# A two-layer DiT block on one core: layer 0's expert rows written to two tables instead of added up in DRAM, with the order of pools and of some small steps changed

## The chip, the cores and the metric

One core of one Trainium2 chip runs the whole program in a single launch. The metric is the device time of that launch in microseconds (us). Before the change three runs took 2960.69, 2967.70 and 2971.63 us; the median is 2967.70 us.

## What is computed

The reference is a diffusion transformer of two layers over 512 image tokens and 256 context tokens of 1024 elements. Each layer is a mixer (retention, window attention and global attention on one wide input product, merged by a gated product) and a mixture of 16 experts of which each token takes two. Six vectors made from the conditioning by a product (shift, scale and gate, twice) modulate both halves. The part that the change is about, shortened:

```
def reference(...):
    for l in range(2):
        mod = silu(c) @ w_mod[l] + b_mod[l]          # image tokens
        mod_c = silu(c_ctx) @ w_mod[l] + b_mod[l]    # context tokens
        sh1, sc1, gt1, sh2, sc2, gt2 = split(mod, 6)
        h = rms_norm(x, g_norm1[l]) * (1 + sc1) + sh1
        hc = rms_norm(ctx, g_norm1[l]) * (1 + csc1) + csh1
        y, yc = mixer_sublayer(h, hc, ...)
        x = x + gt1 * y                              # and ctx in layer 0
        h = rms_norm(x, g_norm2[l]) * (1 + sc2) + sh2
        x = x + gt2 * moe_ffn(h, ...)                # and ctx in layer 0
    return rms_norm(x, g_final)

def moe_ffn(tokens, ...):                            # two experts of one group for each token
    contrib = expert(tokens[t]) * weight             # 2 rows for each token
    return zeros_like(tokens).at[t].add(contrib)
```

## The kernel before

All work is on one core, and each engine works through its instructions in the order in which the program emits them: TensorE (PE) the products, ScalarE (ACT) and VectorE (DVE) the elementwise work, GpSimd (POOL) small statistics, some adds and the indirect DMAs, SyncE (SP) nearly all other DMAs. A wait of one instruction therefore holds up everything behind it on its engine or queue. The 768 tokens are six tiles of 128 (0 to 3 image, 4 and 5 context). A full-precision product is three reduced ones: a weight chunk `raw` (128 x 1024, 512 KB) is cast to `wh` by ACT (L102), DVE makes the rest `wl` (L114), and both `raw` and `xH`/`xL` parts are multiplied (`mm3`). `ws.pump(n)` starts the next n chunks of a fixed list of weights: the load (L83), the cast and the subtraction are emitted where it is called.

Layer 0 ends with its experts. An expert's rows of one block, scaled, are in a tile `yo`; `add_up` (L1667) sends them by an indirect DMA from POOL that adds each row to the token's row of `yd` in DRAM. `yd` has been filled with zeros in layer 0's mixer (six memsets on POOL, six stores on SP, L1134). After the experts comes a loop with a number of turns that is only known on the chip (`For_i`, L1950); no instruction is moved across it. The statement ahead of the loop pumps the 4 x 3 pages of three modulation blocks and two chunks of layer 1's first weights, and then finishes the last expert (`b.finish()`: scale, scatter).

After the loop stands the part that the rows below are about, in this order:

- `fillers(TURN)`: three blocks (1,4), (1,5), (1,6) of layer 1's modulation: products `modps` into four groups of 32 PSUM partitions each (24 matmuls), whose parts (two rows each) DVE adds, four 2 x 512 adds a block (L439). These adds wait in a list `conts` and are emitted by layer 1's mixer. Their results go to DRAM later (`held`).
- `mixer(1)` begins. `n1_load(m)` loads token tile m: `x` (page of pool `kv`, from `xa`) and `y` (page of pool `ot`, from `yd`). `n1_sum(m)` makes x + gt2 * y on DVE (L630, L631) and stores x to `xb` for image tiles (L633, SP). `n1_stat(m)`: sum of squares on ACT (L492), root on POOL (L486, L487). `n1_scale(m)`: ACT (L642). `n1_put(m)`: PE turns the tile (`h1t`, L648), ACT (L665) and DVE (L667) scale and shift it, writing back into the pages of `x` and `y`, and L670/L672 split it into `hH`, `hL`.
- The first product, block AK, goes over the six token tiles (`psAK`); ahead of tile i its step `n1_before` puts tile i+1, loads tile i+5, scales i+2, and takes the statistics of i+3; the sum of tile i+4 is behind it.

Pools of a mixer are opened in the order kv, pp, ot, hp and lie on one another's addresses of the stage before in that order. At the end of layer 1 `last(m)` scales the output tiles: one DVE operation a tile (L1976) with `gf`, the final gain, loaded just ahead of them. A half-width expert block of layer 1 scales its result in two operations of 64 partitions (L1793), since its two halves belong to different columns of the gate row.

Of the kernel before, what the change touches and what calls it, by code (L numbers as in the profile page):

```python
# [16 lines left out]
D = 1024  # L17
# [135 lines left out]
def tile_dit(ctx, tc, a, out):  # L153
# [49 lines left out]
    yd = dram.tile([6 * 128, D], F32, name="yd")  # L203
# [150 lines left out]
    sc0 = small([128, 8, 32], F32, "sc0")  # L354
    jp = pool0.tile([128, 128], I32, tag="pg", name="jp")
# [9 lines left out]
    nc.vector.memset(ones, 1.0)  # L365

# [40 lines left out]
    def mod_gen(l, n, pool, tag, hold=None):  # L407
# [5 lines left out]
        def two():  # L413
            t = pool.tile([2, 1024], F32, tag=tag, name=f"mb{l}_{n}")
            return t[:, 0:512], t[:, 512:1024]

        r, gt = two()
# [8 lines left out]
        ps = acc_tile("modps") if (l, n) in TURN[2:] else oac_tile("modps")  # L426
# [35 lines left out]

        conts.append(fin)
# [12 lines left out]
    held, gt2 = [], []  # L476
# [119 lines left out]
    def mixer(l):  # L596
        att = ExitStack()
        kv = att.enter_context(tc.tile_pool(name=f"kv{l}", bufs=5))
        pp = att.enter_context(tc.tile_pool(name=f"pp{l}", bufs=6))
        ot = att.enter_context(tc.tile_pool(name=f"ot{l}", bufs=4))  # L600
        hp = att.enter_context(tc.tile_pool(name=f"hp{l}", bufs=HP))
# [8 lines left out]
        pages, rs = {}, {}  # L610

        def n1_load(m, first=False):
# [72 lines left out]
        if l:  # L685
# [6 lines left out]
            conts.pop(0)()  # L692
            conts.pop(0)()
# [3 lines left out]
            conts.pop(0)()  # L697
            assert not conts
            n1_sum(1)
            n1_put(0)  # L700
# [3 lines left out]
            n1_stat(1)  # L704
            n1_scale(1)
            n1_sum(2)
# [408 lines left out]
        def soft_gen():  # L1115
# [11 lines left out]
            for i in range(len(steps) + 1):  # L1127
# [509 lines left out]
    def moe(l, R, late, ex, x0):  # L1637
# [284 lines left out]
        for s in range(NE):  # L1922
# [494 lines left out]
```

## Time and profile before

| | |
|---|---|
| median of three runs | 2967.70 us |
| the profiled execution's own time | 2957.83 us |
| its span in the profile | 2956.0 us |
| mean granted TensorE clock | 0.975 of full speed |
| PE busy | 2770.4 us (94%) |
| DVE busy | 1820.3 us (62%) |
| ACT busy | 1279.6 us (43%) |
| POOL busy | 366.2 us (12%) |

PE is busy nearly all the time, so what matters are the few stretches in which it is not. Times in the trace count from the span's start. A timeline row gives the start, the length, engine, line, operation, output and input names, shapes, how many instructions the row joins, and in brackets the idle time of the engine ahead of it with what ended it.

### The profile page before, as it was taken

How to read it: one execution, taken by the hardware profiler on the slowest of the kernel's cores; microseconds unless marked ns; L12 is line 12 of the kernel's file. 1: busy time of each engine (PE TensorE's matmuls, PEld its weight loads, DVE VectorE, ACT ScalarE, POOL GpSimd, SP SyncE). 2: the span in 40 equal slices, each digit the busy share in tenths (PEclk: the TensorE clock that was granted, in tenths of full speed). 3: DMA queues.
4: the chain of work that ended last, by engine and by line, in shares of the span. 5: the costliest groups of instructions: out<-in, count | busy, mean ns of one | idle time of the engine just before them, and what ended most of it. 6: DMA issues, size and time to landing. Idle time of an engine off the chain costs nothing. (4 is left out here: it accounts for less than half of the span.)

```text
span 2956.0 us, 42080 instructions
## 1 busy us (share of the span) xinstructions
PE 2770.4 (94%) x15253; PEld 2221.1 (75%) x15253; DVE 1820.3 (62%) x3235; ACT 1279.6 (43%) x2376; POOL 366.2 (12%) x427
## 2 busy tenths in 40 slices
PE   7999999999999999979999599999999999989985
PEld 3788888888887767767777378888988887767652
DVE  4675567666554455668676576667676655668443
ACT  4444445445443211218566354444455442226332
POOL 1220000000011000023222131100000100012211
PEclk9999999999999999989999799999999999989998
DMA  6433222213243566769999732222223447689997
GB/s 242 132 109 105 90 76 87 95 65 105 99 155 122 194 242 254 263 239 323 340 356 361 254 119 90 83 87 92 72 97 127 143 151 289 214 315 335 372 368 287
DMA packets 203765, 557.63 MB, mean 189 GB/s; under 512 B 27014, under 2 KB 51718, under 8 KB 203552
## 3 DMA queue, kind: packets, MB, share of 16 engines
q1 hardware_dynamic: 175680, 502.59, 47.5%
q0 software_dynamic: 10752, 25.03, 3.4%
q10 hardware_dynamic: 17120, 27.27, 2.5%
q8 instruction: 121, 1.98, 0.3%
q14 instruction: 92, 0.75, 0.1%
HBM read 461.95 MB, written 96.77 MB: 189 GB/s over the span
## 5 line engine op out<-in xcount | busy, mean ns | idle before, releaser
L114 DVE TENSOR_TENSOR wl<-raw,wh 128x1024 fp32r<-128x1024 f32 x474 | 565.3, 1221 | 139.4 <-ACT wh L102 136.2
L102 ACT CAST wh<-raw 128x1024 fp32r<-128x1024 f32 x474 | 484.4, 1050 | 353.7 <-DMA raw<-oT 106.3
L892 ACT ACTIVATE P<-sc,st 128x768 f32<-128x768 f32 (+4 forms) x240 | 176.5, 735 | 339.8 <-DVE st L890 213.3
L890 DVE TENSOR_REDUCE st<-sc 128x1 f32<-128x768 f32 (+4 forms) x240 | 178.6, 744 | 118.9 <-PE sc L179 113.2
L926 ACT CAST ptH<-pt 128x512 fp32r<-128x512 f32 x264 | 143.0, 592 | 124.0 <-PE pt L911 103.3
L179 PE MATMUL psb<-wl,wh 128*128 128x512 f32 x480 | 189.1, 394 | 6.5 <-DVE wl L114 6.5
L179 PE MATMUL psb<-wh,wh 128*128 128x512 f32 x480 | 192.6, 401 | 0.3 <-ACT wh L102 0.3
L179 PE MATMUL psb<-wh,wl 128*128 128x512 f32 x480 | 188.7, 393 | 2.1 <-DVE wl L114 2.0
L936 DVE TENSOR_TENSOR ptL<-pt,ptH 128x512 fp32r<-128x512 f32 x264 | 169.6, 681 | 9.3 <-ACT ptH L926 7.3
L911 PE MATMUL pt<-ident,P 128*128 128x128 f32 x1056 | 141.4, 275 | 14.7 <-ACT P L892 11.8
L911 PEld LDWEIGHTS pt<-ident,P 128*128 128x128 f32 x1056 | 119.7, 140 | 45.4 <-ACT P L892 31.8
L179 PE MATMUL psR<-wh,hH 128*128 128x512 f32 (+1 forms) x384 | 150.7, 392 | 0.0
L179 PE MATMUL psR<-wl,hH 128*128 128x512 f32 (+1 forms) x384 | 147.4, 384 | 3.0 <-DVE wl L114 3.0
L179 PE MATMUL psR<-wh,hL 128*128 128x512 f32 (+1 forms) x384 | 147.8, 385 | 0.0
L898 DVE TENSOR_SCALAR P<-P,st 128x768 f32<-128x768 f32 (+3 forms) x240 | 130.1, 542 | 8.5
L486 POOL TENSOR_SCALAR rstd<-ss 128x4 f32<-128x4 f32 (+2 forms) x70 | 22.6, 323 | 833.9 <-ACT h L492 354.2
L179 PEld LDWEIGHTS psb<-wh,wh 128*128 128x128 f32 x480 | 90.8, 189 | 46.0 <-issue 15.9
L179 PEld LDWEIGHTS psb<-wl,wh 128*128 128x128 f32 x480 | 91.1, 190 | 27.3 <-DVE wl L114 9.8
L179 PE MATMUL sc<-swkT,swqs 128*128 128x256 f32 x704 | 109.1, 281 | 2.2 <-ACT P L892 2.2
L179 PEld LDWEIGHTS psb<-wh,wl 128*128 128x128 f32 x480 | 90.8, 189 | 22.8 <-DVE wl L114 3.7
L1099 DVE COPY sc<-sink 128x1 f32<-128x1 f32 x160 | 25.8, 161 | 128.7 <-PE sc L179 122.5
L179 PE MATMUL yps<-wh,hidT 128*128 128x512 f32 x320 | 105.0, 399 | 0.0
(528 smaller groups left out, 6903.8 us busy)
## 6 DMA issues: line engine op xcount, KB each, us to landing
raw<-in_w_in_dram SPq DMA_DIRECT2D x136, 512.0 KB
raw<-in_w_gate_dram SPq DMA_DIRECT2D x128, 512.0 KB
raw<-in_w_up_dram SPq DMA_DIRECT2D x128, 512.0 KB
raw<-in_w_down_dram SPq DMA_DIRECT2D x128, 512.0 KB
raw<-in_w_mod_dram SPq DMA_DIRECT2D x96, 512.0 KB
raw<-in_w_br_dram SPq DMA_DIRECT2D x48, 512.0 KB
raw<-oT SPq DMA_DIRECT2D x30, 512.0 KB
raw<-in_w_out_dram SPq DMA_DIRECT2D x16, 512.0 KB
```

Of the source, the lines that this page charges most:

```text
L102: self.nc.scalar.copy(c.h, c.raw)
L114: self.nc.vector.tensor_tensor(c.l, c.raw, c.h.bitcast(F32), op=OP.subtract)
L179: nc.tensor.matmul(ps, lhs, rhs, start=start, stop=stop, skip_group_check=share)
L486: nc.gpsimd.tensor_scalar(r[:, 0:cnt], ss, four / n, four * EPS, op0=OP.mult, op1=OP.add)
L890: nc.vector.reduce_max(st[:, 1, h:h + 1], s[:, 0:self.ns], axis=AX.X, negate=True)
L892: nc.scalar.activation(self.P[h][:, 0:self.ns], s[:, 0:self.ns], AF.Exp, bias=st[:, 1, h:h + 1], accum_out=st[:, 2, h:h + 1])
L898: nc.vector.tensor_scalar(self.P[h][:, 0:self.nk], self.P[h][:, 0:self.nk], st[:, 3, h:h + 1], None, op0=OP.mult)
L911: nc.tensor.transpose(pt[:, c * 256 + h * 128:c * 256 + (h + 1) * 128], self.P[2 * x + h][:, i * 128:(i + 1) * 128], ident)
L926: nc.scalar.copy(ph, src)
L936: nc.vector.tensor_tensor(pl, src, ph.bitcast(F32), op=OP.subtract)
L1099: nc.vector.tensor_copy(s[:, nk:nk + 1], sink[:, hd:hd + 1])
```

## The change

1. `yd` has two tables of 768 rows. In layer 0 the scatter only writes: a token's first choice goes to row t of the first table, its second choice to row t of the second. The zero-fill is gone. Layer 1 is as it was.
2. Layer 1's `n1_load` also loads the tile's rows of the second table, as two 128 x 512 halves `y2`, and `n1_sum` adds them to `y`: on DVE for tile 0, on POOL for tiles 1 to 5.
3. The mixer's pools are opened in the order hp, kv, ot, pp.
4. The parts of the three late modulation blocks are copied to SBUF by ACT (128 x 512, L471) and added by one PE product with a 0/1 matrix `four` (`modsum`), so DVE has one add a block. These adds now stand after `n1_scale(1)`, not around `n1_sum(0)`. `n1_stat(1)` moves ahead of `n1_put(0)`.
5. The last expert of layer 0 is finished ahead of the pump, not behind it.
6. In layer 1 the gate row is also kept in the half blocks' layout (`gt2half`), so L1793's two operations become one. `gf` is loaded two experts earlier than the end. The final tiles are multiplied by `gf` first, then scaled by ACT and DVE in turns.

```diff
-    yd = dram.tile([6 * 128, D], F32, name="yd")
+    yd = dram.tile([2 * 6 * 128, D], F32, name="yd")
...
-        ps = acc_tile("modps") if (l, n) in TURN[2:] else oac_tile("modps")
+        ps = acc_tile("modps") if late else oac_tile("modps")
...
         def fin():
-            for i in range(4):
-                nc.vector.tensor_tensor(r, ps[32 * i:32 * i + 2, :], r, op=OP.add)
+            if late:
+                ps2 = oac_tile("modsum")
+                mm(ps2[0:2, :], four, t[:, 512:1024], True, True)
+                nc.vector.tensor_tensor(r, ps2[0:2, :], r, op=OP.add)
...
+        if late:
+            assert v not in (1, 4)
+            nc.scalar.copy(t[:, 512:1024], ps)
         conts.append(fin)
...
+        hp = att.enter_context(tc.tile_pool(name=f"hp{l}", bufs=HP))
         kv = att.enter_context(tc.tile_pool(name=f"kv{l}", bufs=5))
+        ot = att.enter_context(tc.tile_pool(name=f"ot{l}", bufs=4))
         pp = att.enter_context(tc.tile_pool(name=f"pp{l}", bufs=6))
-        ot = att.enter_context(tc.tile_pool(name=f"ot{l}", bufs=4))
-        hp = att.enter_context(tc.tile_pool(name=f"hp{l}", bufs=HP))
...
                 nc.sync.dma_start(pages[m][1], yd[m * 128:(m + 1) * 128, :])
+                for i in range(2):
+                    second[m, i] = half(f"y2{m}{i}")
+                    nc.sync.dma_start(second[m, i], yd[(6 + m) * 128:(7 + m) * 128, i * 512:(i + 1) * 512])
...
                 x, y = pages[m]
+                for i in range(2):
+                    c = slice(i * 512, (i + 1) * 512)
+                    (nc.gpsimd if m else nc.vector).tensor_tensor(y[:, c], y[:, c], second.pop((m, i)), op=OP.add)
                 nc.vector.tensor_tensor(y, y, gt2[m // NIMG], op=OP.mult)
...
-            conts.pop(0)()
-            conts.pop(0)()
             n1_sum(0)
             n1_stat(0)
             n1_scale(0)
-            conts.pop(0)()
-            assert not conts
             n1_sum(1)
+            n1_stat(1)
             n1_put(0)
             for _ in range(2):
                 ws.pump(1)
                 ws.low()
-            n1_stat(1)
             n1_scale(1)
+            assert len(conts) == len(TURN)
+            while conts:
+                conts.pop(0)()
             n1_sum(2)
...
-                if l == 0 and i < 6:
-                    z = half("zeros")
-                    nc.gpsimd.memset(z, 0.0)
-                    nc.sync.dma_start(yd[i * 128:(i + 1) * 128, :].rearrange("p (r c) -> p r c", c=512),
-                                      z[:, None, :].to_broadcast([128, 2, 512]))
...
         def add_up(yo, at, view, rows):
+            how = dict(compute_op=OP.add) if l else {}
...
-                    for n in range(2):
-                        p = slice(n * 64, (n + 1) * 64)
-                        nc.vector.scalar_tensor_tensor(yo[p, 0:512], self.y[p], w[p], gt2row[p, n * 512:(n + 1) * 512],
-                                                       op0=OP.mult, op1=OP.mult)
+                    nc.vector.scalar_tensor_tensor(yo[:, 0:512], self.y, w, gt2half, op0=OP.mult, op1=OP.mult)
...
-            if l == 0 and not nx:
-                ws.pump(4 * len(TURN) + WEND)
             ws.low()
             for b in blocks[s]:
                 b.finish()
+            if l == 0 and not nx:
+                ws.pump(4 * len(TURN) + WEND)
+                ws.low()
+            if l == 1 and s == NE - 3:
+                gf.append(pool0.tile([128, D], F32, tag="pg", name="gf"))
+                nc.sync.dma_start(gf[0], bc(a["g_final"], D))
...
     def last(m):
-        nc.vector.scalar_tensor_tensor(xt[m], xt[m], rs[m][:, 0:1], gf, op0=OP.mult, op1=OP.mult)
+        r = rs[m][:, 0:1]
+        if m % 2:
+            nc.vector.tensor_scalar(xt[m], xt[m], r, None, op0=OP.mult)
+        else:
+            nc.scalar.activation(xt[m], xt[m], AF.Copy, scale=r)
         nc.sync.dma_start(out[0, m * 128:(m + 1) * 128, :], xt[m])
 
     for m in range(NIMG):
         rs[m] = row_rstd(xt[m], y0[m])
+        nc.vector.tensor_tensor(xt[m], xt[m], gf, op=OP.mult)
```

The change moves instructions on three engines after the loop. DVE before, from the third modulation block's adds on (n11m is tile m of layer 1, its `kv` and `ot` the pages of x and y, `gt` the gate row, `mb` a modulation block):

```order
L439 TENSOR_TENSOR mb_6_15628<-modps,mb_6_15628 2x512 x4
L630 TENSOR_TENSOR n111ot<-n111ot,gt_15340 128x1024
L631 TENSOR_TENSOR n111kv<-n111kv,n111ot 128x1024
L667 TENSOR_SCALAR n110ot<-h1t_01_15706,mT_146 128x128 x4
L672 TENSOR_TENSOR hL_0_15716<-n110kv,hH_0_15715 128x512
L672 TENSOR_TENSOR hL_0_15716<-n110ot,hH_0_15715 128x512
L114 TENSOR_TENSOR wl_15738<-raw_15729,wh_15737 128x1024
L630 TENSOR_TENSOR n112ot<-n112ot,gt_15340 128x1024
L631 TENSOR_TENSOR n112kv<-n112kv,n112ot 128x1024
L630 TENSOR_TENSOR n113ot<-n113ot,gt_15340 128x1024
L631 TENSOR_TENSOR n113kv<-n113kv,n113ot 128x1024
L667 TENSOR_SCALAR n111ot<-h1t_11_15772,mT_146 128x128 x4
```

The same place of DVE in the changed kernel, from the split of tile 0 to the put of tile 1 (L682 was L667):

```order
L687 TENSOR_TENSOR hL_0_15714<-n110ot,hH_0_15713 128x512
L114 TENSOR_TENSOR wl_15736<-raw_15727,wh_15735 128x1024
L442 TENSOR_TENSOR mb_4_15599<-modsum,mb_4_15599 2x512
L449 TENSOR_SCALAR mb_4_15599<-mb_4_15599 2x512
L442 TENSOR_TENSOR mb_5_15601<-modsum,mb_5_15601 2x512
L449 TENSOR_SCALAR mb_5_15601<-mb_5_15601 2x512
L442 TENSOR_TENSOR mb_6_15613<-modsum,mb_6_15613 2x512
L645 TENSOR_TENSOR n112ot<-n112ot,gt_15324 128x1024
L646 TENSOR_TENSOR n112kv<-n112kv,n112ot 128x1024
L645 TENSOR_TENSOR n113ot<-n113ot,gt_15324 128x1024
L646 TENSOR_TENSOR n113kv<-n113kv,n113ot 128x1024
L682 TENSOR_SCALAR n111ot<-h1t_11_15784,mT_146 128x128 x4
```

The modulation adds went from ahead of the sums of tiles 0 and 1 to between the chunk's `wl` and the sum of tile 2; the sums of tiles 2 and 3 stand ahead of the put of tile 1 in both.

SP's queue before, from the loads of tile 2 to the first weight:

```order
L623 DMA n112kv<-xa_115 128x1024
L625 DMA n112ot<-yd 128x1024
L623 DMA n113kv<-xa_115 128x1024
L625 DMA n113ot<-yd 128x1024
L633 DMA xb_117<-n110kv 128x1024
L633 DMA xb_117<-n111kv 128x1024
L83 DMA raw_15729<-in_w_in_dram 128x1024
```

The same place in the changed kernel:

```order
L632 DMA n112kv<-xa_115 128x1024
L634 DMA n112ot<-yd 128x1024
L637 DMA y_15670<-yd 128x512
L637 DMA y_15672<-yd 128x512
L632 DMA n113kv<-xa_115 128x1024
L634 DMA n113ot<-yd 128x1024
L637 DMA y_15678<-yd 128x512
L637 DMA y_15680<-yd 128x512
L648 DMA xb_117<-n110kv 128x1024
L648 DMA xb_117<-n111kv 128x1024
L83 DMA raw_15727<-in_w_in_dram 128x1024
```

Sixteen loads instead of eight (tiles 0 to 3) stand ahead of the first store of x, and so ahead of the first weight.

On POOL only the pairs of the root (L486, L487) stood here before, one pair a tile. Now the second table's adds of a tile stand behind the pair of the tile before it:

```order
L496 TENSOR_TENSOR rstd<-rstd,nhalf 128x1
L644 TENSOR_TENSOR n111ot<-n111ot,y_15662 128x512
L644 TENSOR_TENSOR n111ot<-n111ot,y_15664 128x512
L495 TENSOR_SCALAR rstd<-ss 128x1
L496 TENSOR_TENSOR rstd<-rstd,nhalf 128x1
L644 TENSOR_TENSOR n112ot<-n112ot,y_15670 128x512
L644 TENSOR_TENSOR n112ot<-n112ot,y_15672 128x512
```

So POOL can begin the adds of tile m+1 only when tile m's root is done, which needs tile m's sum on DVE and its squares on ACT.

## Rows read from the trace of the kernel before

**Rows 1.** Windows: stretch, us, busy PE, PEld, DVE, ACT, POOL, clock, DMA share, GB/s.
```profile
1350.00:1650.00 300.00, 296.83 (x1566) 216.67 (x1565) 205.39 (x197) 193.89 (x220) 73.72 (x46) 1.00 0.98 350
1650.00:1700.00 50.00, 20.15 (x103) 12.43 (x104) 28.49 (x38) 18.46 (x35) 7.45 (x11) 0.66 0.65 224
...
1750.00:2450.00 700.00, 678.97 (x3994) 589.65 (x3993) 461.58 (x892) 333.17 (x694) 64.20 (x71) 1.00 0.33 110
```

**Rows 2.** Timeline of PE after the loop.
```profile
1660.44 6.72 PE L179 MATMUL modps<-raw,sc 128*32 128x512 f32 x48 [12.63 <-DMA mb<-in_b_mod_dram]
1677.20 1.97 PE L648 MATMUL h1t<-ident,n110ot 128*128 128x128 f32 x8 [10.04 <-ACT n110ot L642]
1683.24 0.79 PE L179 MATMUL psAK<-wh,hH 128*128 128x512 f32 x1 [4.07 <-ACT hH L670]
1690.18 1.97 PE L648 MATMUL h1t<-ident,n111ot 128*128 128x128 f32 x8 [5.29 <-ACT n111ot L642]
...
1704.93 0.47 PE L179 MATMUL psAK<-wh,hH 128*128 128x512 f32 x1 [0.70 <-DVE nAK L790]
```

**Rows 3.** Timeline of SP's queue after the loop.
```profile
1666.38 0.35 SPq L623 DMA_DIRECT2D n110kv<-xa  x1
...
1669.93 0.44 SPq L625 DMA_DIRECT2D n113ot<-yd  x1
1673.87 0.32 SPq L633 DMA_DIRECT2D xb<-n110kv  x1
...
1692.22 0.33 SPq L633 DMA_DIRECT2D xb<-n113kv  x1
```

**Rows 4.** Waits of SP's queue, 1640 to 1700 us: total, times, longest.
```profile
SPq L623 <- PE modps L179: 5.6, 1, 5.6
```

**Rows 5.** Timeline of DVE after the loop.
```profile
1663.81 2.84 DVE L439 TENSOR_TENSOR mb<-modps,mb 2x512 f32<-2x512 f32 x4 [9.47 <-PE modps L179]
...
1672.62 1.23 DVE L631 TENSOR_TENSOR n110kv<-n110kv,n110ot 128x1024 f32<-128x1024 f32 x1
...
1683.83 0.69 DVE L672 TENSOR_TENSOR hL<-n110ot,hH 128x512 fp32r<-128x512 f32 x1
1686.17 1.23 DVE L114 TENSOR_TENSOR wl<-raw,wh 128x1024 fp32r<-128x1024 f32 x1 [1.66 <-ACT wh L102]
...
1692.26 1.37 DVE L667 TENSOR_SCALAR n111ot<-h1t,mT 128x128 f32<-128x128 f32 x4
...
1699.12 1.23 DVE L630 TENSOR_TENSOR n114ot<-n114ot,gt 128x1024 f32<-128x1024 f32 x1 [4.11 <-DMA n114ot<-yd]
```

**Rows 6.** Timeline of ACT around and after the loop.
```profile
1652.98 0.68 ACT L1789 ACTIVATE yo<-ysm,lrec 128x512 f32<-128x512 f32 x1
...
1681.04 1.51 ACT L665 ACTIVATE n110kv<-h1t,mT 128x128 f32<-128x128 f32 x4 [3.89 <-DMA xb<-n110kv]
...
1685.10 1.04 ACT L102 CAST wh<-raw 128x1024 fp32r<-128x1024 f32 x1 [1.39 <-DMA raw<-in_w_in_dram]
```

**Rows 7.** Groups of POOL, whole span: busy us, mean ns, idle before.
```profile
L594 POOL TENSOR_TENSOR oA<-rope,rope 128x512 f32<-128x512 f32 x16 | 21.5, 1343 | 59.0 <-DVE rope L589 35.6 <-issue 12.1 <-DVE st L897 11.3
...
L487 POOL TENSOR_TENSOR rstd<-rstd,nhalf 128x1 f32<-128x1 f32 x26 | 16.2, 625 | 2.2
```

**Rows 8.** Timeline of POOL after the loop.
```profile
1699.17 1.75 POOL L487 TENSOR_TENSOR rstd<-rstd,nhalf 128x2 f32<-128x2 f32 x1
```

**Rows 9.** Timeline of the end, by DVE, SP and ACT.
```profile
2930.64 1.51 DVE L1793 SCALAR_TENSOR_TENSOR yo<-ysm,lrec,gt2row 64x512 f32<-64x512 f32 x2 [5.09 <-PE ysm L179]
...
2937.14 0.35 SPq L1969 DMA_DIRECT2D gf<-in_g_final_dram  x1
2937.54 2.46 SPq L1973 DMA_DIRECT2D cx<-xa  x4
...
2942.91 1.06 ACT L492 ACTIVATE cy<-cx 128x1024 f32<-128x1024 f32 x1 [16.39 <-DMA cx<-xa]
```

**Rows 10.** Timeline of ACT where layer 0's merge begins.
```profile
1000.86 1.05 ACT L102 CAST wh<-raw 128x1024 fp32r<-128x1024 f32 x1 [6.44 <-DMA raw<-oT]
```

More of the change, by code (lines that the diff above doesn't have):

```diff
@@ L354, in tile_dit @@
     sc0 = small([128, 8, 32], F32, "sc0")
+    four = small([128, 2], F32, "four")
     jp = pool0.tile([128, 128], I32, tag="pg", name="jp")
@@ L365, in tile_dit @@
     nc.vector.memset(ones, 1.0)
+    nc.vector.reduce_sum(four, ident.rearrange("p (i r) -> p r i", r=32)[:, 0:2, :], axis=AX.X)
     def late_consts():
@@ L411, in mod_gen @@
         v, half = divmod(n, 2)
[L413 to L417, printed above, removed]
+        late = (l, n) in TURN
+        t = pool.tile([128 if late else 2, 1024], F32, tag=tag, name=f"mb{l}_{n}")
+        r, gt = t[0:2, 0:512], t[0:2, 512:1024]
         b_ap = a["b_mod"][l, n * 512:(n + 1) * 512]
@@ L437, in fin @@
         def fin():
-            for i in range(4):
-                nc.vector.tensor_tensor(r, ps[32 * i:32 * i + 2, :], r, op=OP.add)
+            if late:
[3 more added lines that the diff above has]
+            else:
+                for i in range(4):
+                    nc.vector.tensor_tensor(r, ps[32 * i:32 * i + 2, :], r, op=OP.add)
             if g is not None:
@@ L474, in fillers @@
             yield from g
-    held, gt2 = [], []
+    held, gt2, gf = [], [], []
     def mod_row(pool, tag, l, j, v, name):
@@ L607, in half @@
             return hp.tile([128, 512], dtype, tag="hp", name=name)
-        pages, rs = {}, {}
+        pages, second, rs = {}, {}, {}
         def n1_load(m, first=False):
@@ L1638, in moe @@
         nm = 6 if l == 0 else 4
-        T = nm * 128
+        NY = nm * 128 * (2 - l)
         st = ExitStack()
@@ L1662, in moe @@
             nc.sync.dma_start(gt2row, bc(modd[1][0, 5, :], D))
+            gt2half = mx.tile([128, 512], F32, tag="gt2h", name="gt2half", bufs=1)
+            for i in range(2):
+                src = modd[1][0, 5, i * 512:(i + 1) * 512]
+                nc.sync.dma_start(gt2half[i * 64:(i + 1) * 64],
+                                  bass.AP(tensor=src.tensor, offset=src.offset, ap=[[0, 64], [1, 512]]))
         lrec = mx.tile([128, NE, 4], I32, tag="lrec", name="lrec", bufs=1)
@@ L1666, in add_up @@
         def add_up(yo, at, view, rows):
+            how = dict(compute_op=OP.add) if l else {}
             nc.gpsimd.indirect_dma_start(
                 out=view, out_offset=bass.IndirectOffsetOnAxis(ap=at, axis=0), in_=yo, in_offset=None,
-                bounds_check=rows - 1, oob_is_err=False, compute_op=OP.add)
+                bounds_check=rows - 1, oob_is_err=False, **how)
         class Block:
@@ L1728, in finish @@
                     nc.vector.scalar_tensor_tensor(yo, self.y, w, gt2row, op0=OP.mult, op1=OP.mult)
-                add_up(yo, self.r[:, 1:2], sums, T)
+                add_up(yo, self.r[:, 1:2], sums, NY)
         class Half(Block):
@@ L1790, in finish @@
                 else:
-                    for n in range(2):
-                        p = slice(n * 64, (n + 1) * 64)
-                        nc.vector.scalar_tensor_tensor(yo[p, 0:512], self.y[p], w[p], gt2row[p, n * 512:(n + 1) * 512],
-                                                       op0=OP.mult, op1=OP.mult)
+                    nc.vector.scalar_tensor_tensor(yo[:, 0:512], self.y, w, gt2half, op0=OP.mult, op1=OP.mult)
                 add_up(yo[:, 0:512], rows2[:, self.slot:self.slot + 1],
-                       sums.rearrange("m (h c) -> (m h) c", h=2), 2 * T)
+                       sums.rearrange("m (h c) -> (m h) c", h=2), 2 * NY)
         def words(b, ch):
@@ L1966, in page @@
         return pool0.tile([128, D], F32, tag="pg", name=name)
-    gf = page("gf")
-    nc.sync.dma_start(gf, bc(a["g_final"], D))
+    gf = gf[0]
     xt, y0, rs = {}, {}, {}
@@ L2059, in prepare @@
         nc.gpsimd.iota(self.recs[:, 0:nt, :, 0], pattern=[[128, nt], [0, 2]], base=0, channel_multiplier=1)
-        nc.gpsimd.iota(self.recs[:, 0:nt, :, 1], pattern=[[128, nt], [0, 2]], base=0, channel_multiplier=1)
+        nc.gpsimd.iota(self.recs[:, 0:nt, :, 1], pattern=[[128, nt], [0 if l else 128 * nt, 2]], base=0,
+                       channel_multiplier=1)
         nc.gpsimd.iota(self.eidx, pattern=[[1, NE]], base=0, channel_multiplier=0,
```

1 line of the change is left out of this document (added).

## Prediction

> **What bounds the kernel now.** I read the windows first. In layer 0's experts PE is busy 296.8 of 300 us although the DMA engines are at a share of 0.98, and in layer 1's mixer 679.0 of 700 [rows 1]. Between them lies a hole: from 1650 to 1700 us PE has 20.2 us of work in 50, at a granted clock of 0.66, with neither DMA (0.65) nor DVE (28.5 us) full. That is where the change cuts, so I then read each engine's timeline there. As PE is nearly full for 700 us after the hole and all engines work in program order, what the hole gains or loses should reach the end.
>
> In the timelines I count t from the first modulation product, 1660.44 us [rows 2]. The chain in the hole is one of small steps: products until 6.7; DVE adds (2.84 us for four [rows 5]); the sum of tile 0 ends at 13.4 (1672.62 + 1.23 [rows 5]); squares, root, scale; turn of tile 0 at 16.8 after 10.04 us of idle PE [rows 2]. Then ACT must write into the page of x, and waits 3.89 us until that page's store to `xb` has landed: t = 20.6 [rows 6]. The first AK product starts at 22.8, the turn of tile 1 at 29.7, the AK of tile 2 at 44.5 [rows 2]. The reader should see that the last waits are those for a store, for a weight and for sums on DVE, and none for PE.
>
> **The change in the hole.** SP's first load of a tile waited 5.6 us for the modulation products [rows 4], since its page lies over their weights. With the pools reordered the pages of x and y of tile 0 lie elsewhere, but the halves `y2` now lie there; by the changed program the first of them waits for nearly the last of these products. So SP stands at t = 5.9 as before, only two loads further on. Behind it come 14 loads, not 8, at about 0.45 us of issue each (eight took from 1666.38 to 1670.37 [rows 3]), and all of the tiles 1 to 3 are 1.5 MB, not 1.
>
> Tile 0's sum: the three times four adds are gone from ahead of it, but its two halves must land, and two adds of 0.69 (the row of a 128x512 on DVE [rows 5]) come with two operations of 1.23. With about 9.2 for the landing (5.9 plus 0.9 of issue plus some 2.4 of transfer, my reading) it ends at 13.1. No gain: 13.4 before.
>
> The store of tile 0's x: before, eight loads and it, 4.5 MB, took from 5.9 to 20.6, 14.7 us. Now 5.5 MB are behind the same moment; 1 MB at 350 GB/s, the rate of [rows 1], is 3 us more: t = 23.6 to 24. ACT waits there, PE too. The weight chunk, whose cast began at 24.7 [rows 6], is behind the same queue: 27.5, its `wl` (1.23) ends near 29.4, where before it ended at 27.0. On DVE the moved modulation adds now stand right behind this `wl` (order in the change), and PE has three `modsum` products ahead of the first AK product, which have two PSUM buffers: the third waits for DVE's first add, at about 30.3. AK of tile 0 starts near 30.9 (22.8 before), the turn of tile 1 at 32.2 (29.7).
>
> Sum of tile 2: behind those adds, 32.9 to 35.4; before, the sums of tiles 2 and 3 ran straight ahead of the put of tile 1 at 31.8 [rows 5], so tile 2's from 26.9. Now follows a loop between engines that was not there: DVE sum, ACT squares (1.06 [rows 9]), POOL's root (0.19 to 1.1 and 0.63 in the mean, 1.75 at the longest [rows 7, 8]), POOL's two adds for the next tile, DVE's sum of that tile. A POOL add of two 128x512 tiles takes 1.34 us [rows 7]; two are 2.7. So tile 3's sum comes at 35.4 + 1.2 + 1.5 + 2.7 = 40.9, ends at 43.4, and **tile 1's put stands behind it on DVE**: 43.4, where it was 31.8. That is the largest step, +11.6.
>
> Tiles 4 and 5 load only after tile 3's store of x, which was at 31.8 [rows 3] and is now at 43.5. Tile 4's y was there at 38.7, 6.9 later [rows 5]; with 1 MB more to move between them and behind five weight loads I take 8.3: 51.8, adds to 53.9 (the first overlaps the landing of the second half), sum to 56.4. Tile 2's put waits behind it: 56.4, before 41.1; then hH, hL, and AK of tile 2 at 59.8 in place of 44.5, so +15. Two more tiles go through the same loop, with less to wait for each time, since the 24 products of a tile cover part of it: I take +4 in all, **+19**. Bounds: with POOL's adds free, the same steps give +9.4 (late store, modulation adds, second half's bytes stay); with adds of 1.75, the longest POOL row here, +23.
>
> The Trainium skill's GPSIMD Engine Reference, section 3.1, speaks against putting such adds on POOL: 4497 ns against VectorE's 2293 ns for a fp32 `tensor_tensor` add of 2048 elements a partition, a ratio of 1.96. The trace agrees (1.34 against 0.69 us). By that rule the loss lies in the choice of the engine: with 0.69 us an add the loop through POOL would fall away, and the same chain comes to about +11 instead of +19.
>
> **The other edits.** Finishing the last expert ahead of the pump: `yo` was at 1652.98 behind the casts [rows 6], and the scatter and its landing kept PE until 1660.44 (12.63 us of idle, [rows 2]). It can go 5 us earlier, but the casts then stand behind it, and the `wl` of the last two chunks, which the loop's end also waits for, end about where the scatter landed. I take −0.8, bounds −0.3 and −2.5.
>
> No accumulation in layer 0: the scatter moves less, but PE there is idle 3.2 us of 300 [rows 1]; the windows give it nothing to return but those. 0, bound −3. The zero-fill: stores beside a DMA share far from full there; −0.3, bounds 0 and −1.5.
>
> Pool order in layer 0's merge: its first weights' pages now lie over the mixer's pages that are freed last, ahead of the load that ACT already waits 6.44 us for [rows 10]. A page wait of under a microsecond on that queue: +0.7, bounds 0 and +2.8.
>
> The end: L1793's pair of 1.51 becomes one, −0.75 [rows 9]. `gf` was issued 0.40 us ahead of the four tiles and moves 0.5 MB, 1.5 us at 350 GB/s, ahead of them; now it lands earlier, in time that the last experts leave free: −1.8. The extra multiplication per tile on DVE is beside POOL's roots. Together −2.6, bounds −1.5 and −3.5.
>
> Sum: 19.0 − 0.8 − 0.3 + 0.7 − 2.6 = **+16.0 us**, so the profiled execution's 2957.83 becomes 2973.8. That execution was 9.9 below the median of 2967.7; on the median it is **2983.7**.
>
> **Rivals.**
> 1. *POOL's adds cost no time.* If tiles 1 to 3 are added while the store and the weight are waited for anyway, so that tile 3's sum isn't held up, the +9.4 stays alone: +6.4 in sum, 2974. For it: POOL is idle nearly all of that stretch (7.5 of 50 us, [rows 1]). Against: tile 3's adds stand behind tile 2's root, which needs tile 2's sum.
> 2. *POOL slower beside DVE.* The longest rows here are almost three times the mean [rows 7, 8]. At 1.75 us an add +23 there, +20 in sum, 2988.
> 3. *The hole gets shorter.* Ahead of tile 0's sum three adds of 2.84 and two small ones are gone, and its pages load in the loop's shadow. If the `y2` halves too were in before the products end, sum 0 would end at about 8, five earlier, the store would land before ACT wants it, and each later step would have five to spare: −5 there, −8 in sum, 2960. It decides at one point: whether SP's third load goes out before t = 0 or at 5.9. The pages' places say 5.9.
> 4. *The accumulation was what layer 0's experts waited for.* −3 on top of the rest, 2981. PE's 296.8 of 300 is against more.
>
> **How the numbers follow.** My forecast 0.45, rival 1 0.27, rival 2 0.13, rival 3 0.08, rival 4 0.07. The range takes in rivals 1, 2 and 4 with the bounds of the small terms: 2966 to 2992. Half a per cent, 14.8 us, is about what a measurement of this kernel can tell from no change (the three runs lie within 10.9). Slower by more: rival 2, most of my forecast, whose own range is +10 to +21 (2978 to 2989), and half of rival 4: 0.47. Within: rivals 1, 3, the rest: 0.48. No case gives −14.8; I leave 0.05.
>
> **What would show it.** In the changed profile: PE's idle time between the modulation products and the AK of tile 2, 44.5 before, near 60; SP's wait for those products now at a `y2` load; the put of tile 1 on DVE directly behind the sum of tile 3, and that sum released by POOL's add; POOL's 128x512 adds at 1.3 to 1.4 us; the first cx tiles about 2.6 us sooner after the last product; windows in layer 0's experts unchanged. I am wrong if tile 3's sum isn't released by POOL, if the `y2` loads go out with no wait, or if mixer 1 takes up the loss in slack that the windows hide.

## The result, and the profile after

The changed kernel is slower by about half a per cent: 2981.58 us in the median of 8 runs (2977.34 to 2985.0) against 2962.37 us (2960.69 to 2971.63), ratio 1.0054, 95% interval [1.0042, 1.0065], that is +12 to +19 us with +16 in the middle. The two medians lie 19.2 us apart, at the upper end of that interval. The forecast was +16. Its level, 2983.7, was built on the median of the three runs known then, 2967.70; eight runs have it at 2962.37.

The profiled execution of the changed kernel has a span of 2975.5 us, 19.5 more than before. PE after the loop, to set beside [rows 2] (start, length, what ended the idle time in brackets):

```profile
1648.32 3.65 PE L179 MATMUL ysm<-raw,hidS 128*64 128x512 f32 x16 [0.46 <-ACT hidS L1790]
1663.58 7.42 PE L179 MATMUL modps<-raw,sc 128*32 128x512 f32 x48 [11.61 <-DVEq L1967]
1680.61 1.97 PE L663 MATMUL h1t<-ident,n110ot 128*128 128x128 f32 x8 [9.61 <-ACT n110ot L657]
1682.51 3.03 PE L179 MATMUL modsum<-mb,four 128*2 128x512 f32 x4
1694.79 1.87 PE L179 MATMUL modsum<-mb,four 128*2 128x512 f32 x2 [9.25 <-DVE mb L442]
1698.03 1.28 PE L663 MATMUL h1t<-ident,n111ot 128*128 128x128 f32 x8
...
1722.82 0.77 PE L179 MATMUL psAK<-wh,hH 128*128 128x512 f32 x1 [4.30 <-DVE nAK L804]
```

Counted from the modulation products (1663.58), the turn of tile 1 is at 34.5 (29.7 before) and the AK of tile 2 at 59.2 (44.5 before; forecast 59.8). PE stands for 9.25 us between its second and third `modsum`, waiting for DVE's first modulation add.

SP's queue, timeline and longest waits, beside [rows 3, 4]:

```profile
1664.28 0.36 SPq L632 DMA_DIRECT2D n110kv<-xa  x1
1664.68 0.43 SPq L634 DMA_DIRECT2D n110ot<-yd  x1
1670.21 0.80 SPq L637 DMA_DIRECT2D y<-yd  x2
...
1681.44 0.32 SPq L648 DMA_DIRECT2D xb<-n110kv  x1
...
1706.97 0.33 SPq L648 DMA_DIRECT2D xb<-n113kv  x1
```

```profile
SPq L637 <- PE modps L179: 5.1, 1, 5.1
```

The first two loads go out early, the third (L637) waits 5.1 us for the modulation products, as the pages' places had said. The first store of x goes out at 17.9 (13.4 before).

DVE, beside [rows 5]:

```profile
1676.03 1.23 DVE L646 TENSOR_TENSOR n110kv<-n110kv,n110ot 128x1024 f32<-128x1024 f32 x1
...
1692.92 1.23 DVE L114 TENSOR_TENSOR wl<-raw,wh 128x1024 fp32r<-128x1024 f32 x1 [0.17 <-ACT wh L102]
1694.06 0.67 DVE L442 TENSOR_TENSOR mb<-modsum,mb 2x512 f32<-2x512 f32 x1
...
1697.30 1.20 DVE L645 TENSOR_TENSOR n112ot<-n112ot,gt 128x1024 f32<-128x1024 f32 x1
1698.54 1.23 DVE L646 TENSOR_TENSOR n112kv<-n112kv,n112ot 128x1024 f32<-128x1024 f32 x1
1704.45 1.23 DVE L645 TENSOR_TENSOR n113ot<-n113ot,gt 128x1024 f32<-128x1024 f32 x1 [4.69 <-POOL n113ot L644]
1705.72 1.23 DVE L646 TENSOR_TENSOR n113kv<-n113kv,n113ot 128x1024 f32<-128x1024 f32 x1
1706.86 1.36 DVE L682 TENSOR_SCALAR n111ot<-h1t,mT 128x128 f32<-128x128 f32 x4
...
1717.01 1.23 DVE L645 TENSOR_TENSOR n114ot<-n114ot,gt 128x1024 f32<-128x1024 f32 x1 [7.42 <-POOL n114ot L644]
```

The sum of tile 3 is released by POOL's add after 4.69 us of idle DVE, and the put of tile 1 (L682) stands right behind it, though its own input has been there since 1699.3, when the turn of tile 1 ended. POOL in the same place:

```profile
1701.09 0.19 POOL L495 TENSOR_SCALAR rstd<-ss 128x1 f32<-128x1 f32 x1 [11.95 <-ACT n112ot L501]
1701.37 0.55 POOL L496 TENSOR_TENSOR rstd<-rstd,nhalf 128x1 f32<-128x1 f32 x1
1701.88 2.54 POOL L644 TENSOR_TENSOR n113ot<-n113ot,y 128x512 f32<-128x512 f32 x2
...
1714.45 2.52 POOL L644 TENSOR_TENSOR n114ot<-n114ot,y 128x512 f32<-128x512 f32 x2 [2.58 <-DMA y<-yd]
```

POOL was idle for 11.95 us ahead of tile 2's root. Its adds for tile 3 wait for no load (their row names none); they stand behind that root in its queue. That is the loop of engines that the forecast had counted.

The end, by DVE, SP and ACT, beside [rows 9]:

```profile
2952.74 0.75 DVE L1807 SCALAR_TENSOR_TENSOR yo<-ysm,lrec,gt2half 128x512 f32<-128x512 f32 x1 [5.12 <-PE ysm L179]
...
2958.44 1.88 SPq L1989 DMA_DIRECT2D cx<-xa  x4
...
2961.67 1.06 ACT L501 ACTIVATE cy<-cx 128x1024 f32<-128x1024 f32 x1 [13.09 <-DMA cx<-xa]
```

From the last product to the end it is 22.8 us (2975.5 less 2952.69), 25.4 before (2956.0 less 2930.60).

### The profile page after: what moved, and what is told of

It is laid out like the page before. It is cut to its first block, busy times and chain, and to the rows that moved or that the text cites. A ratio compares the mean times of both kernels' runs of the same rounds, so it can differ in the third digit from the quotient of the medians.

```text
span 2975.5 us, 42115 instructions
## 1 busy us (share of the span) xinstructions
PE 2783.9 (94%) x15259; PEld 2226.2 (75%) x15259; DVE 1810.8 (61%) x3222; ACT 1283.3 (43%) x2381; POOL 351.3 (12%) x431
## 5 line engine op out<-in xcount | busy, mean ns | idle before, releaser
L925 PEld LDWEIGHTS pt<-ident,P 128*128 128x128 f32 x1056 | 119.8, 140 | 44.5 <-ACT P L906 29.9
L179 PEld LDWEIGHTS psb<-wh,wl 128*128 128x128 f32 x480 | 91.2, 190 | 22.8 <-DVE wl L114 3.6
L1113 DVE COPY sc<-sink 128x1 f32<-128x1 f32 x160 | 25.7, 161 | 130.2 <-PE sc L179 123.2
```

The costliest lines, as they stand in the source:

```text
L179: nc.tensor.matmul(ps, lhs, rhs, start=start, stop=stop, skip_group_check=share)
L925: nc.tensor.transpose(pt[:, c * 256 + h * 128:c * 256 + (h + 1) * 128], self.P[2 * x + h][:, i * 128:(i + 1) * 128], ident)
L1113: nc.vector.tensor_copy(s[:, nk:nk + 1], sink[:, hd:hd + 1])
```

## The experiments

Two stretches are compared in every profile. **Hole**: from the start of layer 0's last expert products (`ysm` x16) to the first product of layer 1's second block (`psA`); in the kernel before 1730.28 less 1644.16, 86.1 us. **End**: from the end of the last product to the end of the span, 25.4 us before. The last column is the timed difference to the kernel before, its ratio's interval times 2963 us.

| run | hole | end | both against before | timed, us |
|---|---|---|---|---|
| before | 86.1 | 25.4 | | |
| e5, before again | 85.8 | 25.5 | −0.2 | |
| changed | 103.3 | 22.8 | +14.6 | +16 (12 to 19) |
| e6, changed again | 105.5 | 22.9 | +16.9 | |
| e1, adds on DVE | 96.5 | 23.6 | +8.6 | +8 (4 to 11) |
| e2, loads, no adds | 92.1 | 22.8 | +3.3 | +5 (2 to 9) |
| e3, accumulation back | 85.3 | 22.8 | −3.4 | −4 (−8 to −1) |
| e4, pools only | 84.0 | 25.4 | −2.1 | −1 (−4 to +1) |
| e7, put in the page of y | 102.4 | 24.2 | +15.1 | +17 (12 to 23) |
| e8, e3 with e7's put, adds early | 80.2 | 23.0 | −8.3 | −9 (−12 to −5) |
| e9, ends only | 85.8 | 24.2 | −1.6 | −1 (−3 to +2) |
| e10, modulation back | 105.2 | 23.9 | +17.6 | +17 (12 to 22) |
| e11, sum 3 after put 1 | 99.0 | 24.5 | +12.0 | +12 (7 to 16) |
| e12, e8 with e11's order | 79.3 | 22.8 | −9.5 | −10 (−14 to −6) |

In each timed row the two stretches give the timed difference within its interval. What lies outside them scatters: the last expert product of layer 0 starts at 1644.16 in the first profile of before and at 1647.59 in the second, with one and the same program, and from the first `psA` to the end of the last product it is 1200.3 us in the first and 1206.5 in the second.

**e5 and e6, the two kernels once more.** No edit.

> The kernel before once more, for one profile. The profiles of the changed kernel and of four variants reach the last expert product of layer 0 between 3.7 and 10.4 us later than the one profile of before. Theory (that is scatter between executions): this profile too reaches it 2 to 8 us later than the first, and the stretch from there to layer 1's second product block is as long as in the first within 1 us. Rival (something in the edits costs it, and the first profile is typical): within 1 us of the first at both.

It reached that product 3.4 us later, and the hole was 85.8, both as the theory had them. So the 4.2 us that the changed kernel's profile had lost ahead of the loop (1648.32 against 1644.16) are of the size of this scatter, and no edit is needed to explain them.

> The changed kernel once more, for one profile. Theory: the stretch from the last expert product of layer 0 to layer 1's second product block is 17 us longer than before, as in the first profile of it, within 1 us; the time to that product differs from the first profile's by several us. Rival (the hole itself scatters): more than 3 us apart in the hole.

The product was at 1647.45, 0.9 earlier; the hole was 2.2 us longer than in the first profile, where within 1 was expected. Most of it (1.6) arises in one place, the AK of tile 3 (the first profile, then this one):

```profile
1733.42 0.47 PE L179 MATMUL psAK<-wh,hH 128*128 128x512 f32 x1 [2.59 <-DVE nAK L804]
```

```profile
1733.18 0.76 PE L179 MATMUL psAK<-wh,hH 128*128 128x512 f32 x1 [2.41 <-DVE nAK L804]
```

From there to the turn of tile 5 it is 7.1 us in the first profile and 8.7 in this one. The granted clock from 1733 to 1737 was 1.00 in the first, the higher of its two levels (2.4 GHz), and 0.57 in this one, mostly the lower (1.2 GHz). The hole's length in the changed kernel is known to about 2 us, +17 to +19.

**e1, the second table's adds on DVE.**

```diff
-                    (nc.gpsimd if m else nc.vector).tensor_tensor(y[:, c], y[:, c], second.pop((m, i)), op=OP.add)
+                    nc.vector.tensor_tensor(y[:, c], y[:, c], second.pop((m, i)), op=OP.add)
```

> The changed kernel with all adds of the second table on DVE (0.69 us each) in place of POOL. Theory (the round through POOL is the largest part of the hole's +19): tile 3's sum no longer waits for tile 2's root, put of tile 1 comes about 8 us earlier, the whole about 8 us below the changed kernel, that is about +8 against before. Rival (the late stores and weights behind sixteen loads are the cost, POOL is hidden): within 2 us of the changed kernel.

Ratio 1.0026 [1.0014, 1.0038], +8. DVE there:

```profile
1697.80 1.27 DVE L644 TENSOR_TENSOR n112ot<-n112ot,y 128x512 f32<-128x512 f32 x2
1699.11 1.23 DVE L645 TENSOR_TENSOR n112ot<-n112ot,gt 128x1024 f32<-128x1024 f32 x1
1700.37 1.22 DVE L646 TENSOR_TENSOR n112kv<-n112kv,n112ot 128x1024 f32<-128x1024 f32 x1
1701.51 1.28 DVE L644 TENSOR_TENSOR n113ot<-n113ot,y 128x512 f32<-128x512 f32 x2
1702.83 1.23 DVE L645 TENSOR_TENSOR n113ot<-n113ot,gt 128x1024 f32<-128x1024 f32 x1
1704.09 1.23 DVE L646 TENSOR_TENSOR n113kv<-n113kv,n113ot 128x1024 f32<-128x1024 f32 x1
1705.23 1.36 DVE L682 TENSOR_SCALAR n111ot<-h1t,mT 128x128 f32<-128x128 f32 x4
```

The whole came out as expected. The two sums run without a gap, but the put of tile 1 is 40.4 after the modulation products' start (1664.79) where it was 43.3: 2.9 us earlier, not the 8 expected. The rest comes in the next rounds: the put of tile 2 is 4.4 us earlier (51.4 for 55.8) and that of tile 3 6.8 (59.6 for 66.4). Seven to nine of the 17 to 19 us that the change loses in the hole are the way through POOL.

**e2, the loads without the adds.**

```diff
                 x, y = pages[m]
-                for i in range(2):
-                    c = slice(i * 512, (i + 1) * 512)
-                    (nc.gpsimd if m else nc.vector).tensor_tensor(y[:, c], y[:, c], second.pop((m, i)), op=OP.add)
```

> The changed kernel without the adds: the second table's rows are loaded and left unused, so the second choices of layer 0 are left out of the sum. Theory: the hole keeps +9 of its +19 (more bytes ahead of the first store, modulation adds behind the weight), so the whole is about 10 us below the changed kernel. Rival (it is all the adds): 17 us or more below the changed kernel. Rival (it is all the loads): within 2 us of it.

Ratio 1.0018 [1.0006, 1.003], 11 us below the changed kernel, near the 10 expected; the hole is +5.9 instead of +17 to +19. So 11 to 13 us of the loss in the hole are adds (tile 0's two on DVE among them). With DVE doing all of them they cost 4.4 us (e1's 96.5 less e2's 92.1). The loads alone are 6.7 us: e2's 92.1 less the 85.3 of e3 (next), which has neither. Since e2 leaves out the second choices, layer 1 works on other numbers behind the hole, so its hole says more than its whole time.

**e3, the accumulation back**, with the zero-fill, one table and no second loads; all other edits kept.

```diff
-    yd = dram.tile([2 * 6 * 128, D], F32, name="yd")
+    yd = dram.tile([6 * 128, D], F32, name="yd")
...
-            how = dict(compute_op=OP.add) if l else {}
+            how = dict(compute_op=OP.add)
```

> The changed kernel with the accumulation in DRAM, the zero-fill and the one table back, and all other edits kept. Theory: without the second table the loads go out ahead of the modulation products, the first store is early, and the hole is 3 to 6 us shorter than before; with the end 2.6 and the loop's exit 1.0 shorter, and up to 4 lost ahead of the loop, the whole is 3 to 8 us below before. Rival (the modulation adds' new place and its product cost too): hole as long as before or up to 5 longer, whole from 0 to +5.

Ratio 0.9986 [0.9973, 0.9998]. The whole came out as expected, the hole did not: 0.8 shorter, not 3 to 6, of which the loop's exit is 0.6; the gain of the whole is nearly all from the end. Its first tile is early (turn at 11.8 after the modulation products' start, 16.8 before), and then two waits take most of it back, ACT's for the store of x and PE's for the modulation add (ACT, then PE):

```profile
1687.44 1.50 ACT L674 ACTIVATE n110kv<-h1t,mT 128x128 f32<-128x128 f32 x4 [3.41 <-DMA xb<-n110kv]
```

```profile
1682.12 1.97 PE L657 MATMUL h1t<-ident,n110ot 128*128 128x128 f32 x8 [4.74 <-ACT n110ot L651]
...
1692.95 1.87 PE L179 MATMUL modsum<-mb,four 128*2 128x512 f32 x2 [5.38 <-DVE mb L442]
...
1713.12 0.77 PE L179 MATMUL psAK<-wh,hH 128*128 128x512 f32 x1 [3.86 <-DVE nAK L798]
```

At the AK of tile 2 it is still 1.7 us ahead (42.8 for 44.5). PE has idled 3.86 us there, before 0.70 [rows 2], and its first product takes 0.77 us for 0.47. The granted clock was 0.63 from 1710 to 1715 and 0.69 from 1715 to 1720, in part at the lower level (1.2 GHz), where the kernel before has 1.00 from 1704 to 1730. From this AK to the turn of tile 4 it is 9.5 us (7.9 before), and the lead is gone (52.2 for 52.4).

**e4, the pools alone** in the kernel before.

```diff
+        hp = att.enter_context(tc.tile_pool(name=f"hp{l}", bufs=HP))
         kv = att.enter_context(tc.tile_pool(name=f"kv{l}", bufs=5))
+        ot = att.enter_context(tc.tile_pool(name=f"ot{l}", bufs=4))
         pp = att.enter_context(tc.tile_pool(name=f"pp{l}", bufs=6))
-        ot = att.enter_context(tc.tile_pool(name=f"ot{l}", bufs=4))
-        hp = att.enter_context(tc.tile_pool(name=f"hp{l}", bufs=HP))
```

> The kernel before with nothing but the mixer's pools in the new order. Theory for the 4.2 us that the changed kernel has lost before the loop: page waits in layer 0's merge, so the last expert product of layer 0 is 3 to 4 us later than before, and then the hole is up to 5 us shorter, since the loads no longer wait for the modulation products: whole 0 to -3. Rival (these 4.2 us have nothing to do with the pools): that product within 1 us of before.

Ratio 0.9995 [0.9985, 1.0004]; the hole 2.2 us shorter. Its last expert product came at 1652.40, 8 us later than in the first profile of before, where the theory had 3 to 4 and the rival less than 1. One profile can't decide this: e5 moved by 3.4 with no edit. The timed runs show no loss, but with their interval of −4 to +1 a price of 1 or 2 us ahead of the loop isn't excluded.

**e7, both halves of the put into the page of y.** The transposes have read that page; ACT then doesn't touch the page of x.

```diff
-                    nc.scalar.activation(y[:, c], src, AF.Identity, scale=g, bias=b)
+                    nc.scalar.activation((t if l else y)[:, c], src, AF.Identity, scale=g, bias=b)
...
-            halves = ((slice(0, 512), y), (slice(512, 1024), t))
+            halves = ((slice(0, 512), t if l else y), (slice(512, 1024), t))
```

> The changed kernel with both halves of the put written into the page of y, which PE has read, so that ACT no longer waits for the store of x that reads the other page. Theory (late store is one link of the hole): the put of tile 0 comes 3.5 us earlier; the weight chunk behind it and the modulation adds then limit, so the hole is 1 to 3 us shorter and the whole 1 to 3 us below the changed kernel. Rival (POOL's round sets all of it): no change within 1 us, as tile 3's sum doesn't move.

Ratio 1.0059 [1.004, 1.0078], no gain shown, though 1 to 3 us would be inside the interval; the hole is 0.9 and 3.1 us below the changed kernel's two. ACT's first put came 3.3 us earlier (22.4 after the modulation products' start at 1662.02, 25.7 in the changed kernel), and ACT then waited for the next thing:

```profile
1684.45 1.49 ACT L680 ACTIVATE n110ot<-h1t,mT 128x128 f32<-128x128 f32 x4
...
1689.76 1.04 ACT L102 CAST wh<-raw 128x1024 fp32r<-128x1024 f32 x1 [2.65 <-DMA raw<-in_w_in_dram]
```

The weight is behind the same sixteen loads, and tile 3's sum comes 40.4 after the start, 40.9 in the changed kernel, as the rival had it.

**e10, the modulation adds as before** in the changed kernel, the statistics of tile 1 behind the put of tile 0 with them.

```diff
+            conts.pop(0)()
+            conts.pop(0)()
             n1_sum(0)
             n1_stat(0)
             n1_scale(0)
+            conts.pop(0)()
             n1_sum(1)
-            n1_stat(1)
             n1_put(0)
...
+            n1_stat(1)
             n1_scale(1)
-            while conts:
-                conts.pop(0)()
```

> The changed kernel with the modulation adds as before: four DVE adds a block, around tile 0's sum, no copy and no product, and the statistics of tile 1 where they were. Theory (the new place is one link of the hole's chain): tile 2's sum follows the first weight's subtraction directly, 3.2 us earlier, and what follows comes earlier by as much; tile 0's sum no more than 1 us later, as it waits for its rows; whole 2 to 4 below the changed kernel. Rival (the old adds delay tiles 0 and 1 as much): within 1 us of it.

The rival held: ratio 1.0057 [1.0042, 1.0073], hole 105.2. PE's 9.25 us wait for a modulation add is gone, and tile 2's sum is no earlier: POOL's adds for it now wait for tile 1's root, whose squares stand behind the put of tile 0.

```profile
1692.92 0.19 POOL L487 TENSOR_SCALAR rstd<-ss 128x1 f32<-128x1 f32 x1 [11.80 <-ACT n111ot L493]
...
1693.72 2.48 POOL L636 TENSOR_TENSOR n112ot<-n112ot,y 128x512 f32<-128x512 f32 x2
```

This edit undid several things at once (the adds' place, their form and the statistics' place), so it doesn't price the adds' place alone.

**e11, the sum of tile 3 behind the put of tile 1** in the changed kernel.

```diff
-            n1_sum(3)
             n1_load(4)
...
                 n1_put(i + 1)
+                if l and i == 0:
+                    n1_sum(3)
                 n1_load(i + 5)
```

> The changed kernel with the sum of tile 3 emitted behind the put of tile 1, and so tile 4's loads ahead of tile 3's store. Theory (the put of tile 1 stands on DVE behind a sum that waits for POOL): that put comes 7 us earlier, tile 4's loads 7 us and its sum 5 us earlier; AK of tile 2 then waits for the sum of tile 4 still, so the whole is 4 to 6 us below the changed kernel. Rival (the puts only wait in another place): the hole within 2 us of the changed kernel's.

Ratio 1.004 [1.0025, 1.0054], hole 4.3 and 6.5 us shorter than in the changed kernel's two profiles. DVE:

```profile
1700.98 1.36 DVE L682 TENSOR_SCALAR n111ot<-h1t,mT 128x128 f32<-128x128 f32 x4 [0.20 <-PE h1t L663]
...
1713.55 1.23 DVE L645 TENSOR_TENSOR n114ot<-n114ot,gt 128x1024 f32<-128x1024 f32 x1 [4.65 <-POOL n114ot L644]
...
1715.95 1.36 DVE L682 TENSOR_SCALAR n112ot<-h1t,mT 128x128 f32<-128x128 f32 x4
```

From the modulation products (1664.55) the put of tile 1 is at 36.4 (43.3 in the changed kernel), tile 4's sum at 49.0 (53.4), and the put of tile 2 still stands behind that sum. The order on DVE is shown to be a part of the loss, 4 to 6 us in the hole; the timed middle is 4 below the changed kernel's, with intervals that overlap.

**e9, the edits at the two ends alone** in the kernel before: the early finish, `gt2half`, the early `gf`, the final scaling in turns.

```diff
-            if l == 0 and not nx:
-                ws.pump(4 * len(TURN) + WEND)
             ws.low()
             for b in blocks[s]:
                 b.finish()
+            if l == 0 and not nx:
+                ws.pump(4 * len(TURN) + WEND)
+                ws.low()
+            if l == 1 and s == NE - 3:
+                gf.append(pool0.tile([128, D], F32, tag="pg", name="gf"))
```

> The kernel before with only the edits at the two ends: layer 0's last expert finished ahead of the pump, the gate row in the half blocks' layout, the final gain loaded earlier, the final scaling in turns. Theory: the stretch from the last expert product of layer 0 to the modulation products is 1.0 us shorter, from the last product to the end 2.6 us; the whole 2 to 5 below before. Rival (the time to the loop's exit is taken back by the casts that stand behind): 2.6 alone, the hole unchanged.

Ratio 0.9998 [0.9989, 1.0007]: less than expected. The exit of the loop gained nothing, as the rival had it:

```profile
1664.85 6.81 PE L179 MATMUL modps<-raw,sc 128*32 128x512 f32 x48 [12.68 <-DVEq L1956]
```

12.68 us of idle, 12.63 and 12.18 in the two profiles of before. There SP waits at the loop for the scatter's landing (2.8 and 2.6 us); with the early finish that wait is gone, and what PE's row names is DVE at the loop's end, where the last `wl` ends 15.8 us after the last expert product's start. The end was 1.2 us shorter, not 2.6.

**e8 and e12, versions that beat both kernels.** e8 is e3 with e7's put and the modulation adds ahead of the first weight's pump; e12 has e11's order too.

```diff
+            assert len(conts) == len(TURN)
+            while conts:
+                conts.pop(0)()
             for _ in range(2):
                 ws.pump(1)
                 ws.low()
             n1_scale(1)
-            assert len(conts) == len(TURN)
-            while conts:
-                conts.pop(0)()
```

> The kernel with the accumulation back and all other edits kept, further with both halves of the put written into the page of y, and the modulation adds emitted ahead of the first weight pump. Theory: its hole has two waits left, 3.4 us of ACT for the store of x and 5.4 us of PE for the first modulation add, which stands behind the weight's subtraction; both go, and the weight itself then limits: 4 to 7 us below the variant that only has the accumulation back, so 8 to 11 us below before. Rival (the weight's arrival hides them): within 2 us of that variant, 2 to 6 below before.

> The fastest variant so far (accumulation back, put into the page of y, modulation adds ahead of the pump) with the sum of tile 3 emitted behind the put of tile 1. Theory: the put of tile 1 no longer has 2.5 us of sums ahead of it that PE waits for: 1 to 3 us below that variant, 9 to 12 below before. Rival (DVE is ahead of PE there already): within 1 us of it.

e8: 0.9971 [0.996, 0.9982], 5 us below e3 in the two stretches (4 by the timed middles, whose intervals overlap), both waits gone. PE in e8:

```profile
1684.96 1.02 PE L179 MATMUL modsum<-mb,four 128*2 128x512 f32 x2 [0.17 <-DVE mb L442]
1687.10 1.09 PE L657 MATMUL h1t<-ident,n111ot 128*128 128x128 f32 x8 [0.22 <-ACT n111ot L651]
```

e12: 0.9967 [0.9954, 0.998], the fastest, 2953.55 us in the median. Its step beyond e8, about 1 us, is inside the intervals; it is not shown to be one.

## Why the prediction was right

**The sum.** Forecast +16.0, measured +16 (12 to 19). The forecast of the slower side, of the mechanism and of its place held, and no rival did. That the two numbers are the same is partly luck: the medians are 19.2 apart, the hole of the changed kernel scatters by 2 us, and several terms below missed by 1 to 2 us in opposite directions. (The 44.5 that the forecast's last paragraph calls idle time is the whole time from the start of the modulation products to that AK, work included.)

**The hole, +19.** The two profiles of the changed kernel give +17.2 and +19.4 with the loop's exit in it, forecast +18.2. Step by step, from the start of the modulation products: tile 0's sum ends at 13.7 (forecast 13.1); ACT's put of tile 0 at 25.7 (23.6 to 24); the third `modsum` at 31.2 (30.3); tile 2's sum starts at 33.7 (32.9), tile 3's at 40.9 (40.9); the put of tile 1 at 43.3 (43.4); tile 3's store at 43.4 (43.5); tile 4's sum at 53.4 (53.9); AK of tile 2 at 59.2 (59.8). Two errors cancel. The store was 1.7 to 2.1 us later than 3 us for 1 MB had made it, of which 0.8 were left at tile 2's sum; and the round from tile 2's sum to tile 3's took 0.8 less than forecast, since POOL's root took 0.8 us, not 1.5, and a tile's two adds 2.5, not 2.7. The sum had no term for the granted clock, which moved the hole's length by 1.6 us between two profiles of the same kernel (e6).

**Its two parts.** Forecast: +9.4 with the adds at nothing, +11 with the adds on DVE, both without the loop's exit. Measured from the start of the modulation products to `psA`: +7.3 (e2) and +11.5 (e1); with the exit in it, as in the table, +5.9 and +10.4. The first forecast was too high by 2.1. The put of tile 1 came where its steps put it (37.9 in e2); but tile 4's rows came 7.1 us after tile 3's store, 6.9 before, where 8.3 was taken, and the rounds behind them added little: the puts of tiles 1, 2 and 3 are 6.1, 6.4 and 6.4 later than before. The shares of loads (e2 less e3, 6.7) and adds (11 to 13) are shown; a price of its own for the modulation adds' new place is not. e10 undid it with the order of the statistics and gained nothing, and in e8 their earlier place is together with the put's.

**The ends.** The exit was forecast at −0.8 and came at −0.5 to −1.0 (11.61 and 11.70 us of idle against 12.63 and 12.18), but not for the reason given: with the early finish alone (e9) it is 12.68. Kernels with the plain scatter have 11.3 to 11.7 there, those that accumulate 11.99 to 12.68. That the plain scatter is what helps is read from this grouping, not tried alone. The end's −2.6 was met in the changed kernel (22.8 against 25.4), in part by luck: over all kernels with the same tail it is −0.9 to −2.7. The first output tile's squares begin 9.0 us after the last product, 12.3 before: 3.3 sooner, where 2.6 was forecast (`gt2half` 0.75 us for 1.51, as forecast; the tiles' landing 2.1 sooner, where 1.8 was taken; `gf`'s issue 0.4). The extra multiplication was costed at nothing and takes part of it back, because it is in the way of POOL (last section): from those squares to the end it is 13.8 us in the changed kernel, 13.1 before, and 14.7 to 14.9 in e1, e7, e9, e10 and e11. In e7, e9 and e11 the second tile's multiplication follows the first's at once, and the root's second step is held up too, 1.5 to 1.6 us for 0.57 (e9, DVE, then POOL):

```profile
2949.53 2.44 DVE L1990 TENSOR_TENSOR cx<-cx,gf 128x1024 f32<-128x1024 f32 x2 [9.89 <-DMA cx<-xa]
```

```profile
2950.88 1.52 POOL L487 TENSOR_TENSOR rstd<-rstd,nhalf 128x1 f32<-128x1 f32 x1
```

**The small terms.** The merge's +0.7 and the zero-fill's −0.3 can't be seen: times ahead of the loop vary by several us. For the accumulation forecast 0: PE in the changed kernel is busy 299.0 of 300 us in layer 0's experts, 296.8 before [rows 1]. The 2.2 us between them are the window's end: before, the last product there ended at 1647.81.

```profile
1350.00:1650.00 300.00, 299.01 (x1577) 219.56 (x1577) 207.23 (x199) 195.87 (x221) 56.44 (x47) 1.00 0.93 353
```

The DMA share there fell from 0.98 to 0.93, and nothing came of it that shows: PE was busy nearly all the time in both. That is rival 4's answer too.

**The rivals.** That POOL's adds cost no time (rival 1) fell with e1 and e2. That they are slow beside DVE (rival 2) fell with their 2.5 us for two: DVE stands idle while they run. The shorter hole (rival 3) fell at the point named for it, the third load, which waits 5.1 us for PE; e4 and e3, whose loads go before, show that even then the hole shrinks by 1 to 2 us only: other waits come next, and in e3 the lower clock.

## What to carry to other kernels

A second table instead of an accumulating scatter takes work from a stage that hides it (DMA beside a full PE) and puts it, as loads and adds, on the one stretch where PE has nothing else. Before adding work to such a stretch, write down for each engine what stands ahead of it in its queue: here POOL's add stood behind a root, that root behind a sum, and a put behind the next sum, so twelve adds, ten of them on an engine that was mostly idle (some 1.25 us each), cost 11 to 13 us, and 4.4 with all of them on DVE. And of a chain of waits, one taken away can show little, since the next one is right behind (e7); e8 took two away at once, from another kernel (e3), and had 5 us. Each of these two alone was not tried there.

## What the runs showed of the hardware that was not expected

Executions of one program differ ahead of the change's place: over all profiles the last expert product of layer 0 starts between 1644.2 and 1654.7 us, 3.4 us of it between two profiles of one program, with no order by kernel that so few profiles could show, and the timed runs of before lie between 2956.21 and 2971.63. Single spans can't settle a few microseconds; differences inside a short stretch can.

In the changed tail POOL's small operation lasts as long as DVE's multiplication that began just before it (changed kernel, DVE, then POOL):

```profile
2962.85 1.23 DVE L2001 TENSOR_TENSOR cx<-cx,gf 128x1024 f32<-128x1024 f32 x1 [9.36 <-DMA cx<-xa]
```

```profile
2962.92 1.21 POOL L495 TENSOR_SCALAR rstd<-ss 128x1 f32<-128x1 f32 x1 [7.48 <-DMA cx<-xa]
```

Both end within 0.05 us of each other. The same operation takes 0.19 us where DVE is idle (1701.09 above), and also at this very place in the kernel before, which has no multiplication there:

```profile
2944.15 0.19 POOL L486 TENSOR_SCALAR rstd<-ss 128x1 f32<-128x1 f32 x1 [10.04 <-ACT cy L492]
```

So the root, which the scaling waits for, is a microsecond later: 3.1 us after its squares begin, 2.1 before. The Trainium skill's page SBUF — State Buffer, section "SBUF: two separate sides", says that a DVE operation with two SBUF inputs and a GpSimd operation that reads SBUF exclude each other for the whole instruction; these rows agree with it. No run here kept the changed tail and moved only that multiplication.
